# The second gate moved into the weights of the down-projection, and one multiply-add from PSUM to the row

## The chip, the cores and the metric

The kernel runs on one core of a Trainium2 chip. The metric is device time in microseconds: the median of several executions of the same program. TensorE (PE) multiplies matrices into PSUM, VectorE (DVE) and ScalarE (ACT) read PSUM and the on-chip memory SBUF, GpSimd (POOL) works on SBUF alone, and SyncE (SP) issues the transfers (DMA) to and from the device's memory. Each engine takes its own instructions in order; semaphores make one wait for another.

## The reference, cut to what matters

One layer of a transformer on 2048 tokens of 1024 numbers: a mixer (retention beside attention) and a feed-forward part with squared ReLU. The change touches the last lines:

```python
x = x + g1 * (jnp.concatenate([ret, att], axis=-1) @ w_out)
h2 = _modulate(_rmsnorm(x, norm2_g), sh2, sc2)
x = x + g2 * (jnp.square(jax.nn.relu(h2 @ w_ff1)) @ w_ff2)     # g2: one gate per column, [1024]
return _rmsnorm(x, final_norm_g)
```

`w_ff1` is 1024 x 4096, `w_ff2` 4096 x 1024. The gate `g2` scales the columns of the product, so it may as well scale the columns of `w_ff2`.

## The kernel before, in words

Every f32 operand of the feed-forward products is scaled by a power of two and split into two f16 parts, hi (ScalarE casts) and lo (VectorE subtracts hi from the f32 value); three matmuls (hi hi, hi lo, lo hi) stand for one f32 product. On top of it both products are done two by two blocks at a time by Winograd's form of Strassen's scheme: seven block products instead of eight, with sums of blocks formed beforehand (GpSimd) and sums of results afterwards (VectorE). Hence the sevens below.

**Up stage** (lines 1789 to 1829). The work of TensorE is cut into jobs. A job is 12 matmuls of 128 x 128 by 128 x 512 into one PSUM bank: one of the seven products i, of one block of 256 hidden units (an item n), for one half hf of the tokens. Items 0 to 7 are done for the first half of the tokens, 8 to 15 for both (14 jobs each, halves alternating), and then 0 to 7 for the second half; 220 jobs stand in this stage. `up_out` takes each bank away: product 0 by a ScalarE copy (L1811), the others by a VectorE addition to a kept sum (L1801; product 5 has two additions). Of the seven come four results, each followed by a ScalarE ReLU (L1805) one job later, a GpSimd square (L1806) two jobs later and a store to the device's memory (`store_u`, L1829) four jobs later. The kept sums and results lie in a ring `r` of nine tiles; ten are taken per 14 jobs, and a tile is free again when its store has landed. The PSUM ring has eight banks in this stage.

Beside it the weights of the next item are formed: four sums on GpSimd (L1760), seven hi on ScalarE (L1765), seven lo on VectorE (L1771). And from job 51 of the stage on the down-projection's weights are formed: sixteen blocks m of 256 rows of `w_ff2`, one every 7 jobs (`w2_forms`, through `seven`): two loads of 512 KB, `b` (the first with b11, b12, the second with b21, b22; L1838), four sums t1 to t4 on GpSimd (L1843; t3 is written over b12 and t4 over t1), seven hi on ScalarE (L1848), seven lo on VectorE (L1854), seven stores (L1894). The blocks with even m come at one place in the 14 jobs of an item (t1 in job 1), the blocks with odd m seven jobs on.

**Down stage** (lines 1970 to 2076). 32 pairs p of two token tiles; each has seven products of 12 matmuls (`down`, lines 2006 to 2008). `uf` are the split parts of the up stage's results (hi L1995, lo L1999; sums L1991 on GpSimd). `y` are the two rows (tiles g = 0, 1 of 128 x 1024) to which the product is added; they are loaded, added to and stored again in four rounds rd, each with a quarter of the hidden units. In round 3 the row is normalised and goes out: squares with sums on ScalarE (L2058), a root on GpSimd (L1290, L1291), and one VectorE multiply with the row's root and the final norm's gain (L2073).

`down_out` and `gate` move a result: VectorE adds the bank to kept sums (L2018), GpSimd multiplies the sum by `g2b`, the gate with the scales' inverse in it (L2046), and GpSimd or VectorE adds it to the row (L2048; GpSimd for columns 0 to 511, VectorE for the others).

**What sets the order.** Everything is put into a table by `on(k, phase, ...)`: step k is job k. A loop over k writes out the phases of each step in this order:

```python
FPHASES = ("pe", "sum", "hi", "lo", "relu", "out", "square", "late", "dma")
```

GpSimd's work is in "sum" and "square", ScalarE's in "hi", "relu" and "out", VectorE's in "lo" and "out". A queue is therefore in the order of the jobs, and an instruction that waits holds up all behind it on its engine.

Of the kernel before, what the change touches and what calls it, by code (L numbers as in the profile page):

```python
# [22 lines left out]
P = 128  # L23
D = 1024
# [31 lines left out]
def layer_kernel(ctx: ExitStack, tc: tile.TileContext, a: dict, out: bass.AP):  # L56
# [48 lines left out]
    gs_d = dram.tile([D], F32, name="gs", tag="gs")  # L105
# [13 lines left out]
    scw = const.tile([P, 1], F32, name="scw")  # L119

# [142 lines left out]
    with ExitStack() as st, tc.manual_schedule():  # L263
# [575 lines left out]
        def ff_scales(s):  # L839
# [28 lines left out]
            def scales():  # L868
# [9 lines left out]
                nc.vector.tensor_tensor(c, ma, ms, op=ALU.add)  # L878
                nc.vector.scalar_tensor_tensor(c, w1, 1025.0, c, op0=ALU.mult, op1=ALU.mult)
# [22 lines left out]
                nc.vector.tensor_scalar(g, g, t, w2, op0=ALU.mult, op1=ALU.mult)  # L902
                do(s + 5, "store", lambda: nc.sync.dma_start(gs_d.unsqueeze(0), g[:1]))
# [820 lines left out]
    def open_late():  # L1724
# [8 lines left out]
        nc.sync.dma_start(ff["g2"], gs_d.partition_broadcast(P))  # L1733
# [97 lines left out]
    def seven(b0, source, tiles, low, kinds, scale=None):  # L1831
# [51 lines left out]
    def w2_forms(b0, b):  # L1883
        rd, slot = PLACE[b]

        def tile_of(i):
# [9 lines left out]
            scw,  # L1896
        )
# [37 lines left out]
    def up_jobs():  # L1935
# [18 lines left out]
        on(0, "late", lambda: last3[0](0))  # L1954
        for j in range(4):
# [56 lines left out]
    def down_out(at, p, i):  # L2012

        ps = pu.pop(i)

        def add(x, to=None):
            to = to if to is not None else ff["r"].tile([P, 512], F32, "d")
            nc.vector.tensor_tensor(to, ps, xs_[x], op=ALU.add)  # L2018
            return to

        if i == 0:
            xs_["x"] = ff["r"].tile([P, 512], F32, "d")
            nc.scalar.activation(xs_["x"], ps, AF.Copy)
# [159 lines left out]
```

## Time and profile before

| | us |
|---|---|
| median of 3 runs | 2825.27 (2821.01 to 2826.14) |
| the profiled execution | 2820.49, its span 2818.7 |
| PE, DVE, ACT, POOL busy | 2666.1, 2180.7, 1467.6, 1931.8 |
| up stage, jobs alone | from about 1646 to 2216 |
| of it, with w2's forms | from about 1783 to 2074 |
| down stage, matmuls | from 2216.5 to 2798.9 |

A row of the profile gives line, engine, operation, what is written and what is read, then a count and times. In a row of the timeline the first number is the start in microseconds from the span's start, the second the length; what stands in brackets is how long the engine was idle before, and who released it. A row's length on VectorE or GpSimd includes time in which the instruction has begun and is held up, so distances from start to start say more. In a row of groups the two numbers behind the bar are the total in microseconds and the mean in nanoseconds. In a row with three numbers and slashes they are the least, median and greatest length in nanoseconds. Matmuls overlap: each is listed with 0.38 us, and one starts every 0.216 us.

### The profile page before, as it was taken

Reading aid. Unit: us, or ns where it says so; the run is one execution under the profiler, and the core shown is the slowest. Engines: PE = TensorE matmul, PEld = TensorE weight load, DVE = VectorE, ACT = ScalarE, POOL = GpSimd, SP = SyncE. Lnnn points to the kernel's source line nnn. Section 1 sums busy time; section 2 is a strip of 40 time slices with the busy share of each in tenths; the row PEclk is TensorE's granted clock in tenths of the full one; section 3 lists DMA queues with packets and bytes.
Section 4 is the critical chain, followed back from the end, with each engine's and each line's share of the span. In section 5 each row is a group of like instructions: output and inputs, shape, how many; then the busy total and the mean of one; then the engine's idle time right before and its main releaser. Section 6 shows DMA issues by size and latency. Waiting matters only on the chain.

```text
span 2818.7 us, 46098 instructions
## 1 busy us (share of the span) xinstructions
PE 2666.1 (95%) x16756; PEld 1600.5 (57%) x16756; DVE 2180.7 (77%) x3122; ACT 1467.6 (52%) x2443; POOL 1931.8 (69%) x1499
## 2 busy tenths in 40 slices
PE   6999999997899998999999889999999999999997
PEld 3878788875566665665666544444444444444443
DVE  3678748858987777787777469888876688888898
ACT  2534444425777777777777645555554322222232
POOL 2627428316865668787666679888775688888887
PEclk9999999999999999999999999999999999999998
DMA  6776956827312123333212454777783757575543
GB/s 213 271 258 212 325 216 204 270 100 236 114 43 75 52 66 101 117 93 95 63 61 73 172 163 132 230 249 244 244 275 106 254 180 283 173 275 172 188 142 112
DMA packets 330466, 482.81 MB, mean 171 GB/s; under 512 B 82807, under 2 KB 193655, under 8 KB 325758
## 3 DMA queue, kind: packets, MB, share of 16 engines
q1 hardware_dynamic: 329854, 479.60, 52.0%
q8 instruction: 132, 2.16, 0.3%
q14 instruction: 96, 0.79, 0.1%
q10 hardware_dynamic: 384, 0.26, 0.0%
HBM read 327.57 MB, written 152.20 MB: 170 GB/s over the span
## 4 chain that ended last, share of the span: by engine, by line
PE 57%; DVE 8%; POOL 5%; issue 3%; DMA 2%; ACT 1%; SPq 0%; POOLq 0%; DVEq 0%; ACTq 0%
PE pu L1789 7%; PE pu L1790 7%; PE pu L1791 7%; PE pd L2008 5%; PE pd L2007 5%; PE pd L2006 5%; PE o L239 3%; PE st L205 3%; PE st L206 3%; PE mp L168 2%; DVE nm L181 2%; PE bank L1555 2%; PE bank L1557 2%; PE bank L1556 2%; PE o L238 2%
## 5 line engine op out<-in xcount | busy, mean ns | idle before, releaser
L181 DVE TENSOR_REDUCE nm<-mp 128x1 f32<-128x512 f32 (+1 forms) x576 | 390.7, 684 | 172.3 <-PE mp L168 143.4
L222 POOL TENSOR_TENSOR plo<-p,phi 128x1024 f16<-128x1024 f32 x160 | 353.6, 2211 | 162.6 <-ACT phi L215 130.5
L211 ACT ACTIVATE p<-st 128x512 f32<-128x512 f32 x576 | 338.5, 598 | 197.7 <-PE st L206 122.4
L1789 PE MATMUL pu<-hf,w1f 128*128 128x512 f16 x896 | 340.9, 380 | 0.0
L2008 PE MATMUL pd<-w,uf 128*128 128x512 f16 x896 | 339.6, 379 | 1.3 <-DVE uf L1999 1.2
L1790 PE MATMUL pu<-hf,w1f 128*128 128x512 f16 x896 | 340.7, 380 | 0.0
L1791 PE MATMUL pu<-hf,w1f 128*128 128x512 f16 x896 | 340.6, 380 | 0.0
L2006 PE MATMUL pd<-w,uf 128*128 128x512 f16 x896 | 339.6, 379 | 0.0
L2007 PE MATMUL pd<-w,uf 128*128 128x512 f16 x896 | 339.6, 379 | 0.0
L215 ACT ACTIVATE phi<-p 128x1024 f16<-128x1024 f32 x288 | 303.9, 1055 | 0.0
L1020 PE MATMUL pso<-whi,hlo_l 128*128 128x512 f32 (+1 forms) x768 | 288.4, 376 | 10.6 <-DVE hlo_l L488 10.5
L1018 PE MATMUL pso<-whi,hhi_l 128*128 128x512 f32 (+1 forms) x768 | 296.9, 387 | 0.0
L1019 PE MATMUL pso<-wlo,hhi_l 128*128 128x512 f32 (+1 forms) x768 | 287.1, 374 | 1.7 <-DVE wlo L512 1.7
L238 PE MATMUL o<-wv,plo 128*128 128x65 f16 x2304 | 235.6, 193 | 25.2 <-POOL plo L222 18.1
L224 DVE TENSOR_TENSOR plo<-p,phi 128x512 f16<-128x512 f32 x256 | 240.9, 942 | 16.5 <-ACT phi L215 15.9
L2046 POOL TENSOR_TENSOR d<-d,g2b 128x512 f32<-128x512 f32 x126 | 200.9, 1595 | 69.5 <-DVE d L2018 67.7
L239 PE MATMUL o<-wv,phi 128*128 128x129 f16 x2304 | 243.4, 221 | 0.0
L238 PEld LDWEIGHTS <-plo 128*128 128x128 f16 x2304 | 206.3, 98 | 61.6 <-POOL plo L222 28.2
L1801 DVE TENSOR_TENSOR r<-pu,r 128x512 f32<-128x512 f32 x224 | 151.0, 686 | 111.2 <-PE pu L1791 92.2
L1806 POOL TENSOR_TENSOR r<-r 128x512 f32<-128x512 f32 x128 | 169.0, 1326 | 93.7 <-ACT r L1805 93.3
L205 PE MATMUL st<-qr,ks 128*128 128x512 f16 x576 | 219.6, 381 | 9.8 <-ACT p L211 9.7
L168 PE MATMUL mp<-ks,qr 128*128 128x512 f16 x512 | 196.3, 383 | 30.7 <-DVE nm L181 23.8
(324 smaller groups left out, 6306.3 us busy)
## 6 DMA issues: line engine op xcount, KB each, us to landing
wm<-in_w_ff SPq DMA_DIRECT2D x64, 512.0 KB, 6.7
u<-r SPq DMA_DIRECT2D x128, 256.0 KB, 4.8
ur<-u SPq DMA_DIRECT2D x128, 256.0 KB, 5.7
y<-x SPq DMA_DIRECT2D x64, 512.0 KB, 6.4
wst<-in_w_in SPq DMA_DIRECT2D x60, 512.0 KB, 6.6
wf<-w2f SPq DMA_DIRECT2D x112, 256.0 KB, 3.6
w<-wf SPq DMA_DIRECT2D x28, 1024.0 KB, 10.7
w1r<-in_w_ff SPq DMA_DIRECT2D x48, 512.0 KB, 5.7
```

The costliest lines, as they stand in the source:

```text
L181: nc.vector.tensor_reduce(dst, src, axis=AX.X, op=ALU.max, negate=True)
L205: mm(ps, ks[:, self.g, k], q[:, 0], start=True, stop=False)
L211: nc.scalar.activation(self.p[kt // 2][:, kt % 2], self.s.pop(kt), AF.Exp, scale=HD**-0.5)
L222: nc.gpsimd.tensor_tensor(lo, p, hi, op=ALU.subtract)
L238: mm(o[:, : HD + 1], lo[:, i, c], v[:, : HD + 1], start=False, stop=False)
L239: mm(o, hi[:, i, c], v[:, :VW], start=False, stop=last)
L1789: mm(pu[hf, i], whi, hi, start=k == 0, stop=False)
L1790: mm(pu[hf, i], whi, lo, start=False, stop=False)
L1791: mm(pu[hf, i], wlo, hi, start=False, stop=k == 3)
L2006: mm(ps, u[:, 0, b], w[:, b, 0], start=b == 0, stop=False)
L2007: mm(ps, u[:, 0, b], w[:, b, 1], start=False, stop=False)
L2008: mm(ps, u[:, 1, b], w[:, b, 0], start=False, stop=b == 3)
```

## The change

1. `scales` puts the greatest |g2| into the scale of w2 (a reduction over 128 x 1024 and a multiply on VectorE), and makes one number `scy`, the inverse of all scales of the down product, in place of the row `gs_d` (a multiply over 128 x 1024 and a store). `g2b` in SBUF is now the plain gate.
2. `seven` gets a step `gated` for each of the two loads of a w2 block: the whole load, 128 x 1024 f32, is multiplied in place by `g2b`, the first on GpSimd two jobs before t1, the second on VectorE one job before t1. That is 16 new instructions on each.
3. `down_out` adds a bank to the row or to a kept sum with one scalar_tensor_tensor on VectorE (bank times `scy`, plus the other operand). Sums already known (x, u2, u3) are added to the row by GpSimd beforehand (`known`). GpSimd has per pair four additions instead of four multiplies and two additions, VectorE seven operations out of PSUM as before and no separate additions to the row.
4. The ending: the two partial sums are added in GpSimd's tensor_scalar (VectorE's addition on 128 x 1 goes), and the square, the root and the last multiply are put one or two steps earlier. The mean's 1/1024 is made good by scaling the final gain by 32 once (ScalarE, step 20).

```diff
@@ ff_scales
+                gm = b[:, 8:9]
+                nc.vector.tensor_reduce(gm, x["g", 1], axis=AX.X, op=ALU.max, apply_absolute_value=True)
+                nc.vector.tensor_tensor(w2, w2, gm, op=ALU.mult)
...
-                g, t = x["g", 1], b[:, 8:9]
-                nc.vector.tensor_tensor(t, c, c, op=ALU.mult)
-                nc.vector.tensor_scalar_mul(t, t, 2.0**-24)
-                nc.vector.tensor_scalar(g, g, t, w2, op0=ALU.mult, op1=ALU.mult)
-                do(s + 5, "store", lambda: nc.sync.dma_start(gs_d.unsqueeze(0), g[:1]))
+                nc.vector.tensor_tensor(scy, c, c, op=ALU.mult)
+                nc.vector.scalar_tensor_tensor(scy, scy, 2.0**-24, w2, op0=ALU.mult, op1=ALU.mult)
...
-        nc.sync.dma_start(ff["g2"], gs_d.partition_broadcast(P))
+        nc.sync.dma_start(ff["g2"], gate_d[1].partition_broadcast(P))
...
@@ seven
+            x["raw", g] = w.rearrange("p a b -> p (a b)")
+
+        def gated(g):
+            w, eng = x["raw", g], nc.vector if g else nc.gpsimd
+            eng.tensor_tensor(w, w, ff["g2"], op=ALU.mult)
...
         for g in range(2):
             on(b0 - 5 + g, "dma", fetch, g)
+            if gate:
+                on(b0 - 2 + g, "lo" if g else "sum", gated, g)
...
@@ up_jobs
+        on(20, "late", lambda: nc.scalar.activation(ff["fg"], ff["fg"], AF.Copy, scale=float(D) ** 0.5))
...
@@ down_out
-        def add(x, to=None):
-            to = to if to is not None else ff["r"].tile([P, 512], F32, "d")
-            nc.vector.tensor_tensor(to, ps, xs_[x], op=ALU.add)
-            return to
+        def plus(to, x):
+            nc.vector.scalar_tensor_tensor(to, ps, scy, x, op0=ALU.mult, op1=ALU.add)
...
+        def known(k, g, n, x):
+            d = xs_[x]
+            on(at + k, "square", lambda: nc.gpsimd.tensor_tensor(y[g, n], y[g, n], d, op=ALU.add))
...
         elif i == 1:
-            gate(at, p, 0, 0, add("x"))
+            plus(y[0, 0], y[0, 0])
+            known(1, 0, 0, "x")
+            made(at + 1, p, 0, 0)
         elif i == 2:
-            xs_["u2"] = add("x")
+            plus(new("u2"), xs_["x"])
+            known(1, 0, 1, "u2")
         elif i == 3:
-            xs_["u3"] = add("u2")
+            plus(new("u3"), xs_["u2"])
+            known(1, 1, 1, "u3")
         elif i == 4:
-            gate(at, p, 1, 0, add("u3"))
+            plus(y[1, 0], y[1, 0])
+            known(0, 1, 0, "u3")
+            made(at + 1, p, 1, 0)
         elif i == 5:
-            gate(at, p, 1, 1, add("u3", xs_["u3"]))
-            add("u2", xs_["u2"])
+            plus(y[1, 1], y[1, 1])
+            plus(y[0, 1], y[0, 1])
+            made(at, p, 1, 1)
         elif i == 6:
-            gate(at, p, 0, 1, add("u2", xs_["u2"]))
+            plus(y[0, 1], y[0, 1])
+            made(at, p, 0, 1)
...
@@ gate, now made
-        on(at + 1, "square", lambda: eng.tensor_tensor(c, c, ff["g2"][:, s], op=ALU.mult))
-        eng2 = nc.vector if n or fast else nc.gpsimd
-        on(at + 2, "lo" if eng2 is nc.vector else "square", lambda: eng2.tensor_tensor(y, y, c, op=ALU.add))
...
-        on(at + 3, "relu", square)
+        on(at + 1, "relu", square)
         if n == 1:
-            on(at + 4, "lo", ending, at + 4, p, g)
+            on(at + 1, "relu", ending, at + 1, p, g)
...
@@ ending
-        nc.vector.tensor_tensor(ss[:, :1], ss[:, :1], ss[:, 1:], op=ALU.add)
...
+        def root():
+            nc.gpsimd.tensor_scalar(v, ss[:, :1], ss[:, 1:], D * EPS, op0=ALU.add, op1=ALU.add)
+            nc.gpsimd.tensor_tensor(r, v, half[:, :1], op=ALU.pow)
+
+        on(at, "square", root)
```

What stands in the queues, at three places. First GpSimd in the up stage, around t1 (`bs<-b`) of a block with even m; `r<-r` are squares of the up stage's results, `w1s` sums of the next item's weights, `bs` and `b` the sums of w2. Before:

```order
L1843 TENSOR_TENSOR bs<-b,bs 128x512
L1806 TENSOR_TENSOR r<-r 128x512 x2
L1760 TENSOR_TENSOR w1s<-w1r 128x512
L1806 TENSOR_TENSOR r<-r 128x512
L1843 TENSOR_TENSOR bs<-b 128x512
L1806 TENSOR_TENSOR r<-r 128x512
L1760 TENSOR_TENSOR w1s<-w1r,w1s 128x512
```

After (the sums of w2 now have line 1848):

```order
L1848 TENSOR_TENSOR bs<-b,bs 128x512
L1806 TENSOR_TENSOR r<-r 128x512
L1844 TENSOR_TENSOR b<-b,g2b 128x1024
L1806 TENSOR_TENSOR r<-r 128x512
L1760 TENSOR_TENSOR w1s<-w1r 128x512
L1806 TENSOR_TENSOR r<-r 128x512
L1848 TENSOR_TENSOR bs<-b 128x512
L1806 TENSOR_TENSOR r<-r 128x512
L1760 TENSOR_TENSOR w1s<-w1r,w1s 128x512
```

The new multiply stands between two squares; three squares, whose stores free tiles of the r ring, come behind it.

Second VectorE at the same place; `r<-pu,r` are the additions out of PSUM, `w1f` and `w2f` lo parts. Before:

```order
L1801 TENSOR_TENSOR r<-pu,r 128x512
L1771 SCALAR_TENSOR_TENSOR w1f<-w1s,sc_271,w1f 128x512
L1854 SCALAR_TENSOR_TENSOR w2f<-b,scw,w2f 128x512
L1854 SCALAR_TENSOR_TENSOR w2f<-bs,scw,w2f 128x512
L1771 SCALAR_TENSOR_TENSOR w1f<-w1r,sc_271,w1f 128x512
L1854 SCALAR_TENSOR_TENSOR w2f<-b,scw,w2f 128x512
L1801 TENSOR_TENSOR r<-pu,r 128x512
```

After (the lo parts of w2 now have line 1859):

```order
L1801 TENSOR_TENSOR r<-pu,r 128x512
L1771 SCALAR_TENSOR_TENSOR w1f<-w1s,sc_270,w1f 128x512
L1859 SCALAR_TENSOR_TENSOR w2f<-b,scw,w2f 128x512
L1844 TENSOR_TENSOR b<-b,g2b 128x1024
L1859 SCALAR_TENSOR_TENSOR w2f<-bs,scw,w2f 128x512
L1771 SCALAR_TENSOR_TENSOR w1f<-w1r,sc_270,w1f 128x512
L1859 SCALAR_TENSOR_TENSOR w2f<-b,scw,w2f 128x512
L1801 TENSOR_TENSOR r<-pu,r 128x512
```

The second load's multiply stands in a run of lo parts, between the additions of job 13 and job 2.

Third VectorE at the program's end, from the last lo part on. Before:

```order
L1999 TENSOR_TENSOR uf<-us,uf 128x512
L2048 TENSOR_TENSOR y<-y,d 128x512 x2
L2018 TENSOR_TENSOR d<-pd,d 128x512
L2066 TENSOR_TENSOR ss<-ss 128x1
L2018 TENSOR_TENSOR d<-pd,d 128x512
L2066 TENSOR_TENSOR ss<-ss 128x1
L2073 SCALAR_TENSOR_TENSOR y<-y,cy_e,fgb 128x1024
L2018 TENSOR_TENSOR d<-pd,d 128x512
L2073 SCALAR_TENSOR_TENSOR y<-y,cy_e,fgb 128x1024
L2018 TENSOR_TENSOR d<-pd,d 128x512 x4
L2046 TENSOR_TENSOR d<-d,g2b 128x512
L2048 TENSOR_TENSOR y<-y,d 128x512
```

After:

```order
L2008 TENSOR_TENSOR uf<-us,uf 128x512
L2092 SCALAR_TENSOR_TENSOR y<-y,cy_e,fgb 128x1024 x2
L2027 SCALAR_TENSOR_TENSOR y<-pd,scy,y 128x512
L2027 SCALAR_TENSOR_TENSOR d<-pd,scy,d 128x512 x2
L2027 SCALAR_TENSOR_TENSOR y<-pd,scy,y 128x512 x4
L2092 SCALAR_TENSOR_TENSOR y<-y,cy_e,fgb 128x512 x4
```

The ending of the pair before the last (two multiplies of 128 x 1024) moved ahead of the last pair's banks; the additions to the row and the ss additions are gone.

More of the change, by code (lines that the diff above doesn't have):

```diff
@@ L1829, in store_u, with seven @@
         nc.sync.dma_start(dst, r.rearrange("p (q t) -> p q t", q=4))
-    def seven(b0, source, tiles, low, kinds, scale=None):
+    def seven(b0, source, tiles, low, kinds, scale=None, gate=None):
         x = {}
@@ L1896, in w2_forms @@
             scw,
+            True,
         )
@@ L2014, in down_out, with new @@
         ps = pu.pop(i)
-        def add(x, to=None):
-            to = to if to is not None else ff["r"].tile([P, 512], F32, "d")
-            nc.vector.tensor_tensor(to, ps, xs_[x], op=ALU.add)
-            return to
+        y = {(g, n): ys[p, g][:, n * 512 : (n + 1) * 512] for g in range(2) if (p, g) in ys for n in range(2)}
+        def plus(to, x):
+            nc.vector.scalar_tensor_tensor(to, ps, scy, x, op0=ALU.mult, op1=ALU.add)
+        def new(x):
+            xs_[x] = ff["r"].tile([P, 512], F32, "d")
+            return xs_[x]
@@ L2021, in down_out @@
+        def known(k, g, n, x):
+            d = xs_[x]
+            on(at + k, "square", lambda: nc.gpsimd.tensor_tensor(y[g, n], y[g, n], d, op=ALU.add))
         if i == 0:
[L2022 to L2023 removed]
+            nc.scalar.activation(new("x"), ps, AF.Copy, scale=scy)
         elif i == 1:
[L2025 removed]
+            plus(y[0, 0], y[0, 0])
+            known(1, 0, 0, "x")
+            made(at + 1, p, 0, 0)
```

16 lines of the change are left out of this document (5 added, 11 removed).

## The prediction

> **What bounds the kernel now.** I read the page first, then the stage windows, then TensorE's waits, then the up stage by lines and in order of time.
>
> ```profile
> span 2818.7 us, 46098 instructions
> ...
> 1892.00:1928.00 36.00, 36.00 (x169) 16.32 (x168) 30.95 (x36) 20.39 (x32) 29.02 (x21) 1.00 0.75 251
> ...
> 2500.00:2600.00 100.00, 100.00 (x465) 45.34 (x464) 81.89 (x89) 25.31 (x42) 86.98 (x56) 1.00 0.68 239
> ...
> PE pd L2008 <- DVE uf L1999: 1.2, 2, 0.6
> ```
>
> The busy columns after the length are TensorE, its weight loads, VectorE, ScalarE, GpSimd. In both feed-forward stages TensorE never stops: 100 of 100 us down, 36 of 36 up; its only wait below is 1.2 us in all. So nothing that makes VectorE or GpSimd cheaper in the down stage can gain more than that 1.2 us plus the tail behind the last matmul; and what is added to the up stage must fit beside 36 us in which VectorE is already busy 31 and GpSimd 29. The up stage is where the change puts its new work, so it decides.
>
> ```profile
> 1929.38 1.72 POOL L1843 TENSOR_TENSOR bs<-b 128x512 f32<-128x512 f32 x1
> 1931.05 1.49 POOL L1806 TENSOR_TENSOR r<-r 128x512 f32<-128x512 f32 x1
> 1932.50 1.71 POOL L1760 TENSOR_TENSOR w1s<-w1r,w1s 128x512 f32<-128x512 f32 x1
> 1934.18 1.72 POOL L1843 TENSOR_TENSOR bs<-b,bs 128x512 f32<-128x512 f32 x1
> ...
> 1940.00 1.27 POOL L1843 TENSOR_TENSOR bs<-b,bs 128x512 f32<-128x512 f32 x1 [2.43 <-DVE w2f L1854]
> 1941.23 1.72 POOL L1843 TENSOR_TENSOR bs<-b 128x512 f32<-128x512 f32 x1
> 1946.53 1.04 POOL L1806 TENSOR_TENSOR r<-r 128x512 f32<-128x512 f32 x1 [3.59 <-ACT r L1805]
> 1947.53 1.27 POOL L1843 TENSOR_TENSOR bs<-b,bs 128x512 f32<-128x512 f32 x1
> ...
> 1929.88 1.75 DVE L1854 SCALAR_TENSOR_TENSOR w2f<-bs,scw,w2f 128x512 f16<-128x512 f32 x1
> 1931.56 1.52 DVE L1771 SCALAR_TENSOR_TENSOR w1f<-w1r,sc,w1f 128x512 f16<-128x512 f32 x1
> 1937.84 0.69 DVE L1801 TENSOR_TENSOR r<-pu,r 128x512 f32<-128x512 f32 x1 [1.40 <-DMA u<-r]
> 1939.11 0.74 DVE L1854 SCALAR_TENSOR_TENSOR w2f<-bs,scw,w2f 128x512 f16<-128x512 f32 x1
> 1942.42 0.69 DVE L1801 TENSOR_TENSOR r<-pu,r 128x512 f32<-128x512 f32 x1 [0.60 <-PE pu L1791]
> ```
>
> Alone, a GpSimd sum follows the one before after 1.23 us (1940.00 to 1941.23) and a square after 1.00; a VectorE low part (lo) takes 0.74. Together both stretch: sum to square 1.67, square to sum 1.45, and the lo beside them take 1.75 and 1.52. So an operation of GpSimd and a VectorE operation with two SBUF inputs take turns on something shared, and each lo adds about 0.45 us to a GpSimd operation. The additions out of PSUM (0.69) keep their time.
>
> **The up stage, costed.** A job is 12 matmuls; from 465 in 100 us, 2.59 us. In the 14 jobs of an item with both halves (36.3 us) the code issues on GpSimd 12 sums and 8 squares, and on VectorE 14 additions and 21 lo. Turns taken now: 12 x 1.23 + 8 x 1.00 + 21 x 0.45 = 32.2 of 36.3. It fits, as TensorE's row shows.
>
> ```profile
> L222 POOL TENSOR_TENSOR plo<-p,phi x160: 2118/2132/2696, 643.5 to 1590.4; 128x1024 f16<-128x1024 f32 x160
> L512 DVE TENSOR_TENSOR wlo<-wst,whi 128x1024 fp32r<-128x1024 f32 x60 | 76.5, 1293 | 37.7 <-ACT whi L508 37.1
> u<-r SPq DMA_DIRECT2D x63, 256.0 KB, 5.3
> L1811 ACT ACTIVATE r<-pu 128x512 f32<-128x512 f32 x16 | 9.5, 596 | 12.0 <-PE pu L1791 12.0
> ```
>
> Added per 14 jobs: two multiplies of 1024 on GpSimd, two on VectorE. GpSimd's two-input f32 operation at 1024 is not in the trace: between 2.1 (L222, f16 in and out) and 2.5 (two sums of 512); I take 2.3. VectorE's is L512's 1.29 alone, a turn of 0.45 + (1.29 - 0.74) = 1.0. Turns afterwards: 32.2 + 4.6 + 2.0 = 38.8, over the 36.3 that TensorE needs.
>
> To that comes a wait that grows. The r ring has nine tiles for ten per 14 jobs, so the addition of job 3 and the ScalarE copy of job 1 wait until earlier squares are stored: the square at 1931.05 ended at 1932.54, its store landed 5.3 later, and the addition at 1937.84 already waited 1.40 for it. By the order shown, a 2.3 us multiply now stands ahead of these squares on GpSimd, and a VectorE multiply takes a turn between them. From the start of that multiply, taking turns: 2.3 + 0.45, square 1.45, sum 1.23 + 1.0, square 1.45, sum 1.68, square 1.0 = 10.6; store landed at 15.7 (I take 5.1). VectorE is ready for job 3 at about 15 and holds two more lo behind it, and the sum t4 needs one of them: GpSimd stops from 14.7 to 17.6, with only about 1.3 us of VectorE's turns inside. With that, and a second stop of about 1 us where the first square of the next four waits for its addition, 38.8 becomes 41.4 (bounds: 38.8 with no such loss, 43 with 0.1 us for each of a dozen semaphores between them). So each 14 jobs fall 5.1 us behind TensorE.
>
> What absorbs it: eight PSUM banks. A bank may come free 7 jobs late, 18.1 us, before TensorE stops. The bank most late is that of ScalarE's copy in job 1: without lag job 1 is complete at 1942.42 - 4 x 2.59 = 1932.1, and the copy would end at about 1937.9 (square of job 12 at 1932.2, landing 5.1, copy 0.6): 5.8 late, and 8.3 with the 2.5 that the first two blocks leave. Six more such stretches follow while w2 is formed: 8.3 + 6 x 5.1 = 38.9; less 18.1 is 20.8. TensorE loses about 21 us, in four or five stops between 1890 and 2090; behind them the lag melts (no w2 forms).
>
> ```profile
> PE bank L1587 <- POOL xr L1582: 11.3, 2, 6.9
> ...
> 1646.89 0.63 PE L1789 MATMUL pu<-hf,w1f 128*128 128x512 f16 x1
> 1647.32 0.63 PE L1790 MATMUL pu<-hf,w1f 128*128 128x512 f16 x1
> ```
>
> A stop also slows TensorE: after 6.9 us of waiting the matmuls follow every 0.43 us, not 0.22, for 4.5 us. While VectorE and GpSimd set the pace this is made up within the next stop, so only the last could cost, up to 2.3; I take 0. The Trainium skill, "TensorE: Matmul & The Clock Gate", section "HAM oscillation — how this bites in real kernels", puts the limit at idle gaps of some 3.4 us. By it stops of 5 us would each be followed by half speed, and the sum would be up to 2 us higher.
>
> **The end, costed.**
>
> ```profile
> 2798.52 0.38 PE L2008 MATMUL pd<-w,uf 128*128 128x512 f16 x1
> ...
> 2798.23 0.68 DVE L2018 TENSOR_TENSOR d<-pd,d 128x512 f32<-128x512 f32 x1
> ...
> 2805.39 2.87 DVE L2018 TENSOR_TENSOR d<-pd,d 128x512 f32<-128x512 f32 x4
> ...
> 2810.13 0.63 ACT L2058 ACTIVATE junk<-y 128x512 bf16<-128x512 f32 x1 [0.61 <-DVE y L2048]
> 2810.66 0.18 ACT L2058 ACTIVATION_READ_ACCUMULATOR junk<-y 128x1 f32 x1
> ...
> 2812.46 0.72 POOL L1290 TENSOR_SCALAR cv_e<-ss 128x1 f32<-128x1 f32 x1
> 2813.27 0.94 POOL L1291 TENSOR_TENSOR cy_e<-cv_e,half 128x1 f32<-128x1 f32 x1
> ...
> 2814.24 1.42 DVE L2073 SCALAR_TENSOR_TENSOR y<-y,cy_e,fgb 128x512 f32<-128x512 f32 x2 [0.44 <-POOL cy_e L1291]
> ...
> L1562 DVE SCALAR_TENSOR_TENSOR xr<-bank,sco,xr x32: 739/750/752, 807.8 to 1636.5; 128x512 f32<-128x512 f32 x32
> ...
> L2048 DVE TENSOR_TENSOR y<-y,d 128x512 f32<-128x512 f32 x64 | 108.8, 1702 | 7.1 <-POOL d L2046 7.0
> ```
>
> The last matmul ends at 2798.9, the span at 2818.7: 19.8 us. VectorE is late there: at 2798.23 it adds job 1 of the last pair, at 2805.39 the last four banks, since it waits in line for the endings of the pair before. Per pair two y additions (1.7 each) and the ss additions leave its queue, the seven PSUM additions go from 0.68 to about 0.75 (L1562 has that form); so it reaches the last bank on time. Then: addition 0.8 with its start, square and read-out 0.8 (2810.13 to 2810.84, and a start), root on GpSimd 0.9 to 1.8 (2812.46 to 2814.21 at most), two halves 1.45, and 3.0 from 2815.66 to the end: 7.0 to 7.9. I take 7.6: -12.2. The 1.2 us wait for uf goes with the same lateness: -1.2.
>
> **Edits that I cost at nothing or nearly.**
>
> ```profile
> y<-x SPq DMA_DIRECT2D x64, 512.0 KB, 6.4
> ...
> L908 DVE TENSOR_REDUCE fsb<-fg 128x1 f32<-128x1024 f32 x1 | 1.2, 1220 | 0.0
> ...
> L902 DVE TENSOR_SCALAR fg<-fg,fsb 128x1024 f32<-128x1024 f32 x1 | 0.8, 812 | 0.0
> ```
>
> In the down stage VectorE's additions now wait for GpSimd's known sums one step before; GpSimd has 8 operations per pair for 10, and TensorE has those eight banks, so a late one is hidden unless by 18 us. The y rows are needed two steps earlier: issued four jobs (10.4 us) ahead, landing 6.4 later; late ones meet the same banks. The g2 row is fetched from another buffer, no more bytes; one ScalarE scaling of fg (about 1.05) lies in the up stage, where ScalarE is busy 20 of 36. In the scale step, 0.81 leaves and a reduction of 1.22 comes: +0.4 at most.
>
> Sum: +20.8 - 12.2 - 1.2 + 0.4 = +7.8 us on the profiled 2820.5, which is span and 1.8 around it. The median of the runs shown is 2825.3, 4.8 above that one, so I give 2833. A difference within 0.2% (5.6 us) is about what a measurement here can't tell from none.
>
> **Rivals.** (1) Faster: the lag never fills the banks, and the end's 13 us stay: 2812. That is so if 14 jobs cost under 36.3 + (18.1 - 8.3)/6 = 37.9 us. For it: GpSimd stands idle 7 of 36 us and VectorE 5, and the multiplies of every other block fall into the idle 3.59 at 1946.53. Against it: the 38.8 of turns alone, before any wait. Chance 0.21.
> (2) Partly: the turns saturate but the store wait costs less, 39.4 to 40.9 per 14 jobs; 3 to 4.6 us of lag each, 8 to 18 lost; 2820 to 2831, within 0.2%. Chance 0.19.
> (3) Turns cost the whole recorded duration: 12 x 1.27 + 8 x 1.04 + 21 x 0.74 + 2 x 2.4 + 2 x 1.29 = 46.5, 10 us of lag per stretch, some 50 lost: 2863. Against it, the same arithmetic gives 39.1 for the kernel before, and TensorE doesn't wait. Chance 0.03. This is how the Trainium skill reads, "SBUF — State Buffer", section "Who interferes with whom": the pair of ports is held for the whole instruction and the other engine blocks. The trace agrees on the turns, and its 1.67 instead of 2.0 decides on their length.
>
> My forecast (0.57) holds 2831 to 2843. The range 2811 to 2846 takes in rival (1) at its low end and the upper bound of 43 us per 14 jobs at its high end.
>
> **What would show it.** Right: TensorE waits in the up stage of about 20 us in total for pu banks, released by ScalarE's copy of job 1; VectorE and GpSimd busy over 95% there; waits of VectorE and ScalarE for u<-r stores; a tail of 7 to 8 us; GpSimd below 70% in the down stage. Wrong: TensorE at 100% from 1783 to 2074 (rival 1), or a tail still over 12 us, if GpSimd's known sums hold the last additions.

## The result, and the profile after

The changed kernel takes 2826.8 us (median of 20 runs, 2823.1 to 2830.7), the kernel before 2822.3 (20 runs, 2817.2 to 2826.9): a ratio of 1.0017, 95% interval 1.0011 to 1.0023. It is slower by some 4.5 us, on the side that was forecast. The interval leaves out no change, but the difference is smaller than the 0.2% that the prediction took as the least to be told. 2833 was predicted, with a range of 2811 to 2846. Of the runs behind this page one, of the kernel before with its blocks nine jobs apart, took 3114.1 us at a granted clock of 0.846 and is left out below.

The profiled execution took 2826.9 us. First the head of its page, the stage windows and, of TensorE's waits behind 1600 us, those in the two feed-forward stages (columns as in the prediction: TensorE, its weight loads, VectorE, ScalarE, GpSimd; of a wait the total, the count and the longest).

```profile
span 2825.1 us, 45924 instructions
```

```profile
1892.00:1928.00 36.00, 36.00 (x169) 16.28 (x168) 36.00 (x34) 17.14 (x28) 32.58 (x20) 1.00 0.74 240
2001.00:2037.00 36.00, 32.88 (x150) 14.48 (x149) 36.00 (x33) 18.23 (x28) 33.94 (x21) 1.00 0.68 213
2500.00:2600.00 100.00, 100.00 (x465) 45.36 (x464) 62.06 (x78) 26.15 (x43) 68.49 (x47) 1.00 0.65 240
```

```profile
PE pu L1789 <- DVE r L1801: 8.3, 8, 2.0
PE pu L1791 <- DVE w1f L1771: 2.5, 3, 1.8
```

At 1892 TensorE is still full while VectorE has gone from 30.95 to 36.00 of 36 us: it is behind, and the banks hide it. A hundred microseconds later TensorE has 32.88 of 36. Two waits are new: for a bank (`pu`), 8.3 us, released by VectorE's addition L1801, and at the stage's end for a lo part of w1 (`w1f`), 2.5 us. In the down stage VectorE went from 82 to 62 and GpSimd from 87 to 68 of 100 us, and TensorE, full before but for 1.2 us of waits, had no more than these to gain.

Where the time went, between the two profiled executions:

| stretch | before | after | difference |
|---|---|---|---|
| start to the first weight load of the up stage (L1789) | 1605.0 | 1608.5 | +3.5 |
| up stage, to the first weight load of the down stage | 611.5 | 628.6 | +17.1 |
| down stage, to the end of the last matmul | 582.4 | 580.5 | -1.9 |
| tail behind the last matmul | 19.8 | 7.5 | -12.3 |
| span | 2818.7 | 2825.1 | +6.4 |

The first row can't be told from chance: in the other kernels below, whose code ahead of that point is that of before or of after, this load starts at 1604.5 to 1608.3 (that of before) and at 1602.2 to 1612.2 (that of after). The rest makes +2.9, just under what the medians show (3.1 to 6.5 by the interval).

The second row can be read more sharply from the starts of TensorE's matmuls, one every 0.216 us when nothing is in the way. What the up stage has beyond that is 31.2 us ahead of 1700 us in both kernels (28.3 to 32.7 in the others), and behind it nothing before the change and 16.9 us after it. Of these 9.5 lie at the stops for a bank, 3.0 at those for `w1f`, 3.4 in two stretches at half speed (last section), and 1.0 in small pieces. So the loss is one of the second part of the stage, and up stages as a whole can differ by some 4 us without a cause among the multiplies.

GpSimd in the timeline of the changed kernel, through one period of 14 jobs (start, length, and in brackets the idle time before and who ended it):

```profile
1860.88 2.81 POOL L1844 TENSOR_TENSOR b<-b,g2b 128x1024 f32<-128x1024 f32 x1
...
1878.31 1.27 POOL L1848 TENSOR_TENSOR bs<-b,bs 128x512 f32<-128x512 f32 x1 [1.36 <-DVE w2f L1859]
1879.54 2.80 POOL L1844 TENSOR_TENSOR b<-b,g2b 128x1024 f32<-128x1024 f32 x1
1882.42 1.59 POOL L1848 TENSOR_TENSOR bs<-b 128x512 f32<-128x512 f32 x1
1885.99 1.86 POOL L1806 TENSOR_TENSOR r<-r 128x512 f32<-128x512 f32 x1 [1.98 <-ACT r L1805]
...
1901.12 2.80 POOL L1844 TENSOR_TENSOR b<-b,g2b 128x1024 f32<-128x1024 f32 x1
```

The same place of the next period begins 40.24 us later (40.23 in the others but for the first, 39.35, and two overlapping ones of 41.37, on which more below). TensorE needs 36.3, so VectorE and GpSimd fall 3.9 us behind in each 14 jobs. GpSimd stops twice in it, 1.36 and 1.98 us, for something that VectorE or, through VectorE's addition, ScalarE delivers late. VectorE, at the same time:

```profile
1878.68 1.44 DVE L1859 SCALAR_TENSOR_TENSOR w2f<-bs,scw,w2f 128x512 f16<-128x512 f32 x1
1880.04 0.68 DVE L1801 TENSOR_TENSOR r<-pu,r 128x512 f32<-128x512 f32 x1
1880.64 2.25 DVE L1771 SCALAR_TENSOR_TENSOR w1f<-w1s,sc,w1f 128x512 f16<-128x512 f32 x1
1882.81 1.75 DVE L1859 SCALAR_TENSOR_TENSOR w2f<-b,scw,w2f 128x512 f16<-128x512 f32 x1
1884.48 0.68 DVE L1801 TENSOR_TENSOR r<-pu,r 128x512 f32<-128x512 f32 x1
1885.09 0.73 DVE L1859 SCALAR_TENSOR_TENSOR w2f<-b,scw,w2f 128x512 f16<-128x512 f32 x1
1885.74 1.21 DVE L1844 TENSOR_TENSOR b<-b,g2b 128x1024 f32<-128x1024 f32 x1
```

A lo that meets GpSimd's multiply takes 2.25 us, beside a sum 1.75, alone (GpSimd idle, 1885.09) 0.73. GpSimd's multiply takes 2.81 with a hold-up of 0.45 in it, so 2.36 alone (the shortest recorded one, in the kernel before with the multiplies, is 2.36); VectorE's follows to the next start after 1.14.

The tail of the changed kernel, from the last matmul on:

```profile
2817.24 0.38 PE L2017 MATMUL pd<-w,uf 128*128 128x512 f16 x1
```

```profile
2817.65 0.75 DVE L2027 SCALAR_TENSOR_TENSOR y<-pd,scy,y 128x512 f32<-128x512 f32 x1 [1.11 <-PE pd L2017]
2818.32 1.41 DVE L2092 SCALAR_TENSOR_TENSOR y<-y,cy_e,fgb 128x512 f32<-128x512 f32 x2
2818.50 0.63 ACT L2075 ACTIVATE junk<-y 128x512 bf16<-128x512 f32 x1 [1.80 <-DVE y L2027]
...
2819.32 0.57 POOL L2086 TENSOR_SCALAR cv_e<-ss 128x1 f32<-128x1 f32 x1 [1.57 <-ACT junk L2075]
2819.97 0.56 POOL L2087 TENSOR_TENSOR cy_e<-cv_e,half 128x1 f32<-128x1 f32 x1
2820.57 1.41 DVE L2092 SCALAR_TENSOR_TENSOR y<-y,cy_e,fgb 128x512 f32<-128x512 f32 x2 [0.84 <-POOL cy_e L2087]
```

VectorE now waits for the last bank (1.11 us idle) in place of having four of them in line, and has it 0.8 us behind the last matmul, not 9.4 (2808.3 in the kernel before, by the rows of the prediction). Bank, square, root, two halves and the last store then follow closely, 6.7 us for 10.4 before, since the gate's multiply and the addition to the row are no longer in that chain. So the 12.3 us are 8.6 of lateness and 3.7 of chain.

### The profile page after: what moved, and what is told of

It is laid out like the page before. It is cut to its first block, busy times and chain, and to the rows that moved or that the text cites. A ratio compares the mean times of both kernels' runs of the same rounds, so it can differ in the third digit from the quotient of the medians.

```text
span 2825.1 us, 45924 instructions
## 1 busy us (share of the span) xinstructions
PE 2670.2 (95%) x16756; PEld 1599.4 (57%) x16756; DVE 2117.6 (75%) x3057; ACT 1467.4 (52%) x2444; POOL 1887.2 (67%) x1453
## 5 line engine op out<-in xcount | busy, mean ns | idle before, releaser
L1789 PE MATMUL pu<-hf,w1f 128*128 128x512 f16 x896 | 342.1, 382 | 8.4 <-DVE r L1801 8.3
L2035 POOL TENSOR_TENSOR y<-y,d 128x512 f32<-128x512 f32 x128 | 210.6, 1647 | 138.8 <-ACT uf L2004 91.4
L238 PE MATMUL o<-wv,plo 128*128 128x65 f16 x2304 | 234.7, 193 | 25.4 <-POOL plo L222 18.1
L224 DVE TENSOR_TENSOR plo<-p,phi 128x512 f16<-128x512 f32 x256 | 242.4, 948 | 16.5 <-ACT phi L215 15.9
L205 PE MATMUL st<-qr,ks 128*128 128x512 f16 x576 | 219.8, 382 | 10.3 <-ACT p L211 10.2
L206 PE MATMUL st<-qr,ks 128*128 128x512 f16 x576 | 219.6, 381 | 0.1
L239 PEld LDWEIGHTS <-phi 128*128 128x128 f16 x2304 | 205.0, 97 | 19.6
```

The source lines that it names most:

```text
L238: mm(o[:, : HD + 1], lo[:, i, c], v[:, : HD + 1], start=False, stop=False)
L239: mm(o, hi[:, i, c], v[:, :VW], start=False, stop=last)
L1789: mm(pu[hf, i], whi, hi, start=k == 0, stop=False)
```

## The experiments

Two theories stood at the start. **Turns**: operations of GpSimd and VectorE's operations with two SBUF inputs share something, the sum of their turns per 14 jobs is the pace, the PSUM banks absorb a part of the lag. **VectorE's queue**: VectorE is simply full, and what GpSimd does matters only by its hold-ups. "Pace" below is the time from a step of the w2 forms to the same step 14 jobs later, and "up stage" the stretch of the table above.

### Without the multiplies, and the multiplies alone

The first kernel is the changed one without the 32 multiplies, so its gate is missing from the output:

```diff
-            if gate:
+            if False:
```

> The changed kernel without the 32 multiplies of w2 by the gate (so the gate is left out of the result); all else, the end and the down stage too, stays changed. Theory A (the multiplies overfill the turns that VectorE and GpSimd take in the up stage, and that alone costs the 17 us there): TensorE at 100% through the stage in which w2 is formed, no wait for pu banks, VectorE back to about 31 of 36 us; the tail stays at 7.5 us; time 12 to 15 us under the kernel before. Theory B (a part of the loss is in the new order of the rest, or in the scale step, since the first job of the up stage starts 3.5 us later than before): the start of the up stage still 3 us late and the gain only 9 to 11 us.

Measured: 2808.6 us, ratio 0.9946 (0.9933 to 0.9960). No `pu` wait at all, up stage 610.3 us. The second is the kernel before with the 32 multiplies (the gate is then applied twice):

```diff
+            x["raw", g] = w.rearrange("p a b -> p (a b)")
+
+        def gated(g):
+            w, eng = x["raw", g], nc.vector if g else nc.gpsimd
+            eng.tensor_tensor(w, w, ff["g2"], op=ALU.mult)
...
+            if scale is not None:
+                on(b0 - 2 + g, "lo" if g else "sum", gated, g)
```

> The kernel before with nothing but the 32 multiplies added, at the same places in the up stage (so the gate enters twice). Theory A: the up stage as in the changed kernel, VectorE busy 36 of 36 us there, waits for pu banks, 15 to 19 us lost; tail still about 20 us; time 15 to 19 us over the kernel before. If the loss hangs on the changed down stage or the earlier loads: under 10 us. Theory B: the first job of the up stage as early as in the kernel before.

Measured: 2839.4 us, ratio 1.0057 (1.0042 to 1.0072), up stage 627.3, and the waits of the changed kernel, in TensorE's waits of this one:

```profile
PE pu L1789 <- DVE r L1801: 9.8, 12, 2.0
PE pu L1791 <- DVE w1f L1771: 3.5, 4, 1.8
PE pd L2015 <- DVE uf L2006: 1.2, 2, 0.6
```

So the change falls into two parts: the multiplies cost 0.57% (16 us), all in the up stage, and the rest of the change gains 0.54% (15 us), the tail and the 1.2 us of `uf` waits, which this kernel keeps. Together they would make +0.03%, with an interval of about 0.2% either way, for the 0.17% of the whole change.

### Both multiplies on one engine

```diff
-            w, eng = x["raw", g], nc.vector if g else nc.gpsimd
+            w, eng = x["raw", g], nc.gpsimd
...
-                on(b0 - 2 + g, "lo" if g else "sum", gated, g)
+                on(b0 - 2 + g, "sum", gated, g)
```

> The changed kernel with both multiplies of a block on GpSimd (32 there, none on VectorE). Theory A (turns are the bound): GpSimd's turns rise by 2.3 where VectorE's fall by 1.0 per block, so 2.6 us more per 14 jobs, up to 15 us more lost than in the changed kernel. Theory V (VectorE's queue is the bound, since it is busy 36.4 of 36.4 us while GpSimd idles 3): the stage becomes faster, by 1 to 2 us per 14 jobs, and the time comes down 6 to 12 us.

Measured: 2837.2 us, ratio 1.0043 (1.0030 to 1.0057), up stage 638.1, pace 41.6 (41.3 to 41.9 from one period to the next, and one of 42.4 left out). Taking work from VectorE made it worse, so VectorE's own work isn't the whole of it. The other way round, both on VectorE:

```diff
-            w, eng = x["raw", g], nc.vector if g else nc.gpsimd
+            w, eng = x["raw", g], nc.vector
...
-                on(b0 - 2 + g, "lo" if g else "sum", gated, g)
+                on(b0 - 2 + g, "lo", gated, g)
```

> The changed kernel with both multiplies of a w2 block on VectorE; the arithmetic is complete. Turn theory: a GpSimd multiply holds the shared path for 2.36 us, a VectorE one adds about 1.0 to the turns, so 14 jobs cost 2 x (2.36 - 1.0) = 2.7 us less than the 40.2 us measured: about 37.5, a lag of 1.2 per 14 jobs, which the eight banks absorb. No pu waits, the time about 11 us below the kernel before (2812). Rival, VectorE's own queue: it was busy in 36.4 of 36.4 us with two multiplies, so four make it later by another 2 x 1.3 us and more per 14 jobs: pu waits of 30 us and more, the time about 20 us above the kernel before (2843).

Measured: 2826.0 us, ratio 1.0006 (0.9996 to 1.0016), up stage 629.7, pace 40.13: neither 2812 nor 2843. Both expectations missed. The two starts of VectorE's multiply at the same place of two periods, and GpSimd in between:

```profile
1857.56 2.29 DVE L1844 TENSOR_TENSOR b<-b,g2b 128x1024 f32<-128x1024 f32 x1
...
1897.69 2.29 DVE L1844 TENSOR_TENSOR b<-b,g2b 128x1024 f32<-128x1024 f32 x1
```

```profile
1873.31 1.27 POOL L1848 TENSOR_TENSOR bs<-b,bs 128x512 f32<-128x512 f32 x1 [3.88 <-DVE w2f L1859]
1878.27 1.27 POOL L1848 TENSOR_TENSOR bs<-b 128x512 f32<-128x512 f32 x1 [3.69 <-DVE b L1844]
1879.62 1.36 POOL L1806 TENSOR_TENSOR r<-r 128x512 f32<-128x512 f32 x1
1882.21 1.28 POOL L1848 TENSOR_TENSOR bs<-b,bs 128x512 f32<-128x512 f32 x1 [1.23 <-DVE b L1844]
```

GpSimd's sums now wait for VectorE's multiplies and lo parts, and while GpSimd stands still no turn of its own is taken. What moved off GpSimd came back as its idle time.

### One of the two multiplies left out

Each kernel leaves one load ungated, so that the output lacks half of the gate. First without GpSimd's, then without VectorE's:

```diff
-            if gate:
+            if gate and g:
```

> The changed kernel without the sixteen GpSimd multiplies (the first load of each w2 block is not gated, VectorE still gates the second). Turn theory: 2.36 us less per 14 jobs than 40.2, so 37.8; a lag of 1.5, absorbed, no pu waits. Theory that VectorE's own queue sets the pace and a GpSimd operation costs it only the time by which it holds up the lo beside it (2.25 us instead of 0.74, so 1.5): 40.2 - 1.5 = 38.7, a lag of 2.4, the up stage some 6 us less long than the changed kernel's.

```diff
-            if gate:
+            if gate and not g:
```

> The changed kernel without the sixteen VectorE multiplies (the second load of each w2 block is not gated, GpSimd still gates the first). Turn theory: 1.0 less per multiply and one multiply of each kind per block, so 2 x 1.0 less per 14 jobs at most, 38.2 to 39.2. VectorE's queue: its multiplies take 1.98 and 1.13 us of its time from start to start, 3.1 in all, so 40.2 - 3.1 = 37.1: a lag of 0.8, absorbed, no pu waits; the multiply on VectorE is then the dearer of the two, which is the opposite of the turn theory's order.

In the first of these expectations there is a slip: each 14 jobs have two multiplies of each kind, so the two theories should have read 40.2 - 4.7 (35.5, which TensorE's 36.3 would hide) and 40.2 - 3.0 (37.2). Measured: 36.63 without GpSimd's (between the two) and 38.21 without VectorE's (the turn theory's 38.2, not 37.1). A multiply is worth 1.8 us of pace on GpSimd and 1.01 on VectorE. The turn theory's order of the two holds (2.36 and 1.0), though GpSimd's is worth less than that; VectorE's queue would have them about equal (1.5 and 1.55). There is a single time of each, 2812.2 and 2809.1 us, and the argument rests on the traces; no wait for a bank in either, 1.0 us for `w1f` in the second; up stages 610.2 and 613.1.

The five kernels together. The rows are windows of one period each, ahead of TensorE's first stop for a bank, of, in this order, the changed kernel, both on GpSimd, both on VectorE, without GpSimd's, without VectorE's:

```profile
1860.88:1901.12 40.24, 40.24 (x188) 18.32 (x187) 40.24 (x38) 20.91 (x32) 36.82 (x24) 1.00 0.70 223
```

```profile
1865.58:1907.02 41.44, 41.44 (x193) 18.78 (x192) 40.12 (x36) 20.24 (x32) 41.44 (x26) 1.00 0.66 213
```

```profile
1857.56:1897.69 40.13, 40.13 (x188) 18.19 (x186) 40.13 (x41) 20.26 (x32) 30.62 (x21) 1.00 0.70 223
```

```profile
1880.63:1917.26 36.63, 36.63 (x172) 16.56 (x171) 36.63 (x38) 20.18 (x32) 31.37 (x20) 1.00 0.77 245
```

```profile
1873.15:1911.36 38.21, 38.21 (x178) 17.31 (x177) 38.21 (x36) 20.04 (x31) 35.45 (x24) 1.00 0.73 234
```

VectorE is never idle in four of the five, but its busy time has the hold-ups in it, so a full VectorE by itself speaks for neither theory. Turns by the prediction's prices (32.2 without multiplies, 2.36 and 1.0 for one on GpSimd and on VectorE); GpSimd's idle time is what it leaves of the window above:

| multiplies per 14 jobs | turns | pace measured | excess | GpSimd idle |
|---|---|---|---|---|
| 4 GpSimd | 41.6 | 41.6 | 0.0 | 0.0 |
| 2 GpSimd, 2 VectorE (changed kernel) | 38.9 | 40.23 | 1.3 | 3.4 |
| 2 GpSimd | 36.9 | 38.21 | 1.3 | 2.8 |
| 2 VectorE | 34.2 | 36.63 | 2.4 | 5.3 |
| 4 VectorE | 36.2 | 40.13 | 3.9 | 9.5 |

Where GpSimd never stands still the pace is the sum of the turns, to the 0.3 us by which single periods differ. Each microsecond in which it waits for VectorE adds about 0.4 (0.38 to 0.47) to that sum. A likely reason, not shown, is that VectorE fills the rest of the gap with work that would have had its turn anyway. The figure is read off the table, not derived, and GpSimd's idle time was measured, not forecast; a kernel that the table doesn't use bears it out below. So the turn theory stands with this addition. The queue theory alone falls by the kernel with both multiplies on GpSimd: there VectorE has less to do, and 1.3 us to spare in the period shown, and the pace is longer.

### Fewer banks, and a longer r ring

Six PSUM banks in the up stage for eight:

```diff
-                        ff["ps"].extend(pool(late_ff, "fp3", space=PSUM), "p", 2)
+                        pass
```

> The changed kernel with six PSUM banks in the up stage in place of eight; the arithmetic is complete. If a growing lag is absorbed by the banks and the rest is lost, two banks less absorb 2 x 2.59 = 5.2 us less: the up stage about 5 us longer, the time about 2832, and the first stop about one and a half blocks earlier. If the stops are single late events that the ring has nothing to do with, no change (2827).

Measured: 2828.2 us, ratio 1.0020 (1.0010 to 1.0029). TensorE's first wait for a bank:

```profile
1916.19 0.38 PE L1789 MATMUL pu<-hf,w1f 128*128 128x512 f16 x1 [0.25 <-DVE r L1801]
```

and in the changed kernel:

```profile
1966.81 0.38 PE L1789 MATMUL pu<-hf,w1f 128*128 128x512 f16 x1 [0.24 <-DVE r L1801]
```

The first stop comes 50.6 us earlier, 1.26 periods; 5.2 us of bank at 3.9 us of lag per period is 1.3 periods. So the banks absorb a lag that grows evenly (the expectation gave one and a half blocks; 1.26 periods are two and a half, since a period has two). But the up stage grew by 2.1 us, not 5.2. This kernel has no wait for `w1f`, the changed one has 2.5 us of it: near the stage's end its TensorE runs into w1's lo parts, which stand in the same late queue. By the starts of the matmuls the stops for a bank cost 14.2 us here and 9.5 in the changed kernel, 4.7 more and near the 5.2 expected; the 3.0 at `w1f` are gone, and the rest is 0.6 more. So the two extra banks were worth less than half of what they could hold, because what they save in one wait comes back in the other.

Ten tiles in the r ring for nine, one less for w:

```diff
-        ff["w"].extend(pool(late_ff, "fw2", side="right"), "w", 3)
-        ff["r"].extend(pool(late_ff, "fr2", side="right"), "r", 5)
+        ff["w"].extend(pool(late_ff, "fw2", side="right"), "w", 2)
+        ff["r"].extend(pool(late_ff, "fr2", side="right"), "r", 6)
```

> The changed kernel with ten tiles in the r ring in place of nine (the w ring has eight in place of nine to make room); the arithmetic is complete. If the wait for stores of r costs the 2.6 us per 14 jobs that the prediction gave it, the lag per 14 jobs falls to about 1.3 us and the banks absorb nearly all of it: pu waits vanish, the time about 2812. If turns alone make the lag, the period of 40.2 us per 14 jobs and the time stay as in the changed kernel (2826 to 2828).

Measured: 2825.4 us, ratio 1.0007 (0.9996 to 1.0019), up stage 628.9, and in GpSimd's timeline the pace of the changed kernel:

```profile
1858.08 2.81 POOL L1844 TENSOR_TENSOR b<-b,g2b 128x1024 f32<-128x1024 f32 x1
...
1898.31 2.81 POOL L1844 TENSOR_TENSOR b<-b,g2b 128x1024 f32<-128x1024 f32 x1
```

The r ring and its stores have next to no part in the loss. In the changed kernel VectorE waits once for a store while w2 is formed:

```profile
1957.75 0.69 DVE L1801 TENSOR_TENSOR r<-pu,r 128x512 f32<-128x512 f32 x1 [1.46 <-DMA u<-r]
```

It is in the time of the periods of 41.37 us. With ten tiles there is no such wait, and every period from 1796 us on has 40.21 to 40.25; behind 1700 us TensorE loses 15.8 us, 1.1 less than in the changed kernel, which the times of the two can't tell apart.

### The blocks farther apart

Nine jobs between blocks of w2 instead of seven, in the changed kernel (its arithmetic is complete):

```diff
-            w2_forms(first1 + 1 + 7 * m, b)
+            w2_forms(first1 + 1 + 9 * m, b)
```

> The changed kernel with one w2 block formed every 9 jobs and not every 7; nothing left out. Theory A: per 14 jobs with both halves the turns come to 16.1 + 14/9 x 11.4 = 33.8 us, under the 36.3 of TensorE; behind job 164, where an item has 7 jobs, 24.2 + 17.7 = 41.9, for 33 jobs, so some 13 us of lag, which eight banks take. No or nearly no wait for pu banks; time 9 to 14 us under the kernel before, so faster than both. If VectorE's queue has another cause to be late (store waits of the r ring), waits stay and the gain is under 6 us.

Measured: 2811.9 us, ratio 0.9959 (0.9946 to 0.9971). It beats both kernels. In its windows TensorE is full where the changed kernel has 134.69 of 145 us:

```profile
1965.00:2110.00 145.00, 145.00 (x674) 65.71 (x672) 138.75 (x134) 73.16 (x113) 125.36 (x79) 1.00 0.75 242
```

The up stage is 614.4 us, with 3.2 us of waits for `w1f` left. The same line in the kernel before (9 for 7 there) is the control:

> The kernel before with a block of w2 every 9 jobs in place of 7; the arithmetic is complete. If the spacing only gives room to work that did not fit, the kernel before, whose TensorE does not wait there, gains nothing: 2823 to 2825, and the whole gain of the spaced changed kernel is its end. If the spacing itself saves time, it falls by several microseconds here too.

Measured: 2821.0 us, ratio 0.9999 (0.9987 to 1.0011). Spacing gives nothing where nothing is late; what the spaced kernel has gained is the end. Eight jobs in the changed kernel:

> The changed kernel with a block of w2 every 8 jobs in place of 7; the arithmetic is complete. A block takes VectorE 40.2 / 2 = 20.1 us and gets 8 x 2.59 = 20.7: no lag grows, the time is that of the spacing of nine, about 2812. If the loss came from the order of the queues inside 14 jobs and not from the sum of the work, the shifted places give some other loss, between 2812 and 2830.

Measured: 2817.2 us, ratio 0.9982 (0.9973 to 0.9991), up stage 619.5: between the two, and the expectation of no lag missed. GpSimd's multiply at the same place 56 jobs (seven blocks) apart:

```profile
1866.74 2.81 POOL L1844 TENSOR_TENSOR b<-b,g2b 128x1024 f32<-128x1024 f32 x1
...
2017.61 2.81 POOL L1844 TENSOR_TENSOR b<-b,g2b 128x1024 f32<-128x1024 f32 x1
```

```profile
PE pu L1791 <- DVE w1f L1771: 6.4, 5, 2.8
```

That is 150.9 us, and TensorE needs 145.1. The expectation took half a period as the price of a block, but a period also holds 14 jobs' own additions, squares and w1 forms. In 56 jobs the changed kernel has eight blocks and needs 4 x 40.23 = 160.9; seven blocks need 150.9; so a block costs 10.0 us and 56 jobs without one 80.9. It fits when 145.1 - 80.9 = 64.2 us hold the blocks: 6.4 in 56 jobs, one every 8.7. Nine is beyond that, eight is not, as measured. (This is an estimate with two points and a third, nine, that agrees.)

The same 56 jobs put the rule of the five kernels to a test, since the table doesn't use them:

```profile
1866.74:2017.61 150.87, 150.87 (x701) 68.39 (x700) 150.65 (x141) 75.34 (x117) 134.36 (x84) 1.00 0.67 218
```

Their turns are 4 x 16.1 for the 14 jobs without a block and 7 x 11.4 for the blocks (both prices stand in the expectation for nine jobs), 144.2 us; GpSimd is idle for 16.5. The excess is 6.7 us, 0.4 of the idle time, as before.

### The order of the ending

The changed kernel with its last squares and endings as late as before:

```diff
-        on(at + 1, "relu", square)
+        on(at + 3, "relu", square)
...
-            on(at + 1, "relu", ending, at + 1, p, g)
+            on(at + 3, "relu", ending, at + 3, p, g)
```

> The changed kernel with the last squares and the endings put back to three steps behind the result, as late as before the change; the arithmetic is complete. If VectorE's lighter queue (no additions to the row) makes the gain at the end, the tail behind the last matmul stays at about 8 us and the time at about 2827. If the earlier place of the endings makes it, the two multiplies of 128 x 1024 of the pair before stand among the last banks again, the tail grows by 3 to 6 us, and the time to 2830 to 2833.

Measured: 2826.0 us, ratio 1.0014 (1.0004 to 1.0024). Its last matmul and the last bank:

```profile
2812.97 0.38 PE L2017 MATMUL pd<-w,uf 128*128 128x512 f16 x1
```

```profile
2813.39 0.75 DVE L2027 SCALAR_TENSOR_TENSOR y<-pd,scy,y 128x512 f32<-128x512 f32 x1 [1.11 <-PE pd L2017]
```

The span is 2820.8, so the tail is 7.4 us, as in the changed kernel, and VectorE waits the same 1.11 us for the last bank. So the earlier endings by themselves give nothing. What is left of the change there is VectorE's lighter queue and the shorter chain, 8.6 and 3.7 us by the rows; the heavier queue with the early endings was not tried.

## Why the prediction was right, and where it was not

The side and the mechanism were those forecast. The case that came out is rival (2), though: its pace (39.4 to 40.9), its loss (8 to 18 us) and its time (2820 to 2831) hold what was measured, 40.23, 17.1 and 2826.8, and for its reason, a store wait that costs less. It had 0.19, the forecast's own 2831 to 2843 had 0.57. Of the signs named, the tail, VectorE over 95% (322.1 of 327 us from 1783 to 2110) and GpSimd under 70% in the down stage came; the waits for banks were 8.3 us and not some 20, GpSimd was busy 91% of those 327 us and not over 95%, and of the waits for stores VectorE had one.

**The up stage decides: right.** TensorE stays full in the down stage, and 17 of the 20.8 us forecast were lost in the up stage. Leaving the multiplies out gives that back, and adding them to the kernel before brings it.

**Turns over the 36.3 us: right, and priced well.** 38.8 were forecast; 38.9 come out with the multiply as measured (2.36 for the 2.3 assumed), and the kernel with all four on GpSimd has the sum of the turns as its pace, 41.6. Rival (3), in which each operation holds the other for its whole length, would have needed 46.5 and is out: the pace is 40.23.

**"A wait that grows" (the store of the r ring): wrong.** This term was to bring 38.8 to 41.4. The stores landed in 4.4 us (4.8 before, medians of the whole run), VectorE waited for one of them, 1.5 us, and a tenth tile took that away and left the pace at 40.23. What stands in its place is GpSimd's waiting for VectorE, 3.4 us per period (1.36 for a lo part before a sum is written over its input, 1.98 for a square whose addition is late), which costs about 0.4 of itself: 1.3 us. The two stops were forecast in kind, of 2.9 and 1 us, but with the wrong cause for the first. So the lag is 3.9 per 14 jobs, not 5.1.

**What absorbs it: right in kind, mis-sized.** The first stop moved with the number of banks as a steady lag asks. But the banks were not all that stopped TensorE: at the stage's end it also met w1's late lo parts, and lost 3.0 us there. With 3.9 per period, the 8.3 and 18.1 of the prediction would give 8.3 + 6 x 3.9 - 18.1 = 13.6 us; 17.1 were lost. Some of the missing 3.5 is that second limit. The half speed behind the stops isn't: the kernel before with the multiplies has no such stretch behind a bank stop of 2 us, and loses 17.6 us behind 1700 us where the changed kernel, with two, loses 16.9. How much the 8.3 is off stays open. That 17.1 came near the 20.8 forecast is in part luck: the lag was put 7.2 us too high over six periods, and the rest of the sum some 3.5 too low. The bank most late was not the one named: each stop was released by VectorE's additions (L1801), none by ScalarE's copy of job 1.

**The end: right.** -12.2 forecast, -12.3 measured (7.6 and 7.5 us of tail). The order of the endings alone isn't the cause, as putting them back showed; VectorE's lateness makes 8.6 of it and the shorter chain 3.7.

**The down stage: right.** -1.2 forecast; the waits for `uf` are gone and the stage is 1.9 shorter. GpSimd's sums ahead hold nothing up.

**The scale step (+0.4 at most): not to be seen** in a start of the up stage that moves by several microseconds from one kernel to the next without a cause in its code.

**The number.** 2833 for 2826.8: 3.0 of the 6.2 come from the base (three runs of before had a median of 2825.3, twenty have 2822.3), 3.7 from the up stage, and 0.8 from the down stage and the tail, all the same way. That is 7.5; the 1.3 the other way lie in the start of the up stage and in the profiled executions, which aren't the medians. The 2846 at the high end of the range is some 3 us more than the 43 us per 14 jobs that it is said to stand for: 8.3 + 6 x 6.7 - 18.1 is 30.4, and with 13 us less at the end that makes 2843.

## What to carry to other kernels

Where two engines take turns on a path, add up the turns of both per unit of TensorE's work, and set the sum against TensorE's time: above it the excess grows with every repetition until the buffers are full, so 3.9 us too much in a period of 36.3 became 17 at the end. A sum below it isn't enough by itself: with both multiplies on VectorE the turns were 36.2, and the waiting of one engine for the other made the period 40.13. Then look at when the work is due: the same multiplies at nine jobs a block instead of seven cost 3 us (2811.9 for the 2808.6 without them), while moving them all to VectorE brought nothing, because GpSimd, relieved, stood waiting for it, and moving them all to GpSimd cost 10 us more. And before crediting an earlier place in the order with a gain, put it back alone.

## What the hardware showed that was not expected

After some stops of only 2 us TensorE ran at half speed. In the changed kernel's timeline:

```profile
2036.85 0.38 PE L1789 MATMUL pu<-hf,w1f 128*128 128x512 f16 x1 [1.98 <-DVE r L1801]
2037.07 0.55 PE L1790 MATMUL pu<-hf,w1f 128*128 128x512 f16 x1
2037.41 0.63 PE L1791 MATMUL pu<-hf,w1f 128*128 128x512 f16 x1
2037.84 0.63 PE L1789 MATMUL pu<-hf,w1f 128*128 128x512 f16 x1
...
2040.39 0.46 PE L1789 MATMUL pu<-hf,w1f 128*128 128x512 f16 x1
2040.69 0.38 PE L1790 MATMUL pu<-hf,w1f 128*128 128x512 f16 x1
```

For 3.3 us the matmuls follow every 0.43 us. The same happened behind a stop of 1.98 us at 2077.08, but not behind one of 1.96 at 1996.61. In the seven kernels with stops for a bank, 8 of those of 1.96 to 2.2 us slow TensorE and 12 don't, and one of 3.09 (both multiplies on GpSimd, at 1961.92) didn't. So the length alone doesn't decide. The Trainium skill, "TensorE: Matmul & The Clock Gate", section "What's actually happening", says that how busy TensorE has been is judged in a window of about 3.4 us, which runs freely and doesn't start anew with the kernel. A window of that kind, which a stop of 2 us fills more or less according to where it falls, would fit these cases, but no run shows where the window stood. That a stop under 3.4 us can be enough, and that the slow stretch lasts 3.3 us, is what the trace adds. The prediction thought of half speed behind stops of 5 us; here the stops were shorter and still cost up to 8 x 0.21 = 1.7 us each. That was made up while VectorE and GpSimd set the pace: behind 1996.61, without a slow stretch, two more stops of 0.19 and 0.87 us follow before the next long one, and behind 2036.85, with one, none does.
